# A hybrid decoder step on one core: the 16x16 diagonal blocks of a triangular inverse move from TensorE doubling steps to VectorE

## The chip, the cores and the metric

One Trainium2 chip, one of its cores. The metric is device time of one execution in microseconds (us); of several runs the median is given.

## The reference, cut to what matters

The kernel computes one inference step of a two-layer decoder trunk for 256 prompt rows and 8 sample rows. Each layer has a mixer (four mLSTM heads and eight gated-delta-rule heads behind one input projection), a cross attention and a SwiGLU. The part that the change touches is the chunked delta rule of the prompt:

```python
A = jnp.where(strict[None, :, :, None], decay_ts * kk * bc[:, None, :, :], 0.0)
eg = jnp.exp(g)
rhs = vc - eg[..., None] * jnp.einsum('bthd,bhde->bthe', kc, S)
U = lax.linalg.triangular_solve(jnp.transpose(A, (0, 3, 1, 2)), jnp.transpose(rhs, (0, 2, 1, 3)),
                                left_side=True, lower=True, unit_diagonal=True)
wu = bc[..., None] * jnp.transpose(U, (0, 2, 1, 3))
```

The system is unit lower triangular. The reference solves it in chunks of 64 rows; the kernel uses chunks of 128 rows, so that there are two chunks per head, and multiplies by an explicit inverse.

## The kernel before, in words

All weights stream from HBM in blocks of 128x1024 numbers. For each block `block` issues a DMA into `raw`; ScalarE (ACT) rounds it to `wh`; VectorE (DVE) forms the remainder `wl = raw - wh`; and `stream` on TensorE (PE) multiplies `wh` and `wl` with the rounded activations and their remainder (`xh`, `xl`), three matmuls of 264 columns for each pair of 128x128 tiles, 24 matmuls for a block. `wh` and `wl` have three buffers each, so a block can be prepared only once the block three before it is used up. These two operations carry a high priority.

Everything else of a layer runs as Python generators ("chains") beside these streams. A chain writes its next few instructions and yields a number; `pump`, called between the matmuls of a stream, resumes a chain once an estimated PE clock has passed that number of nanoseconds. PE's order is thus exactly the order in which the program writes its instructions (`manual_schedule`); each PE instruction stands in the stream where its chain was resumed, and PE waits there if its operands aren't ready. The orders on DVE, ACT and POOL are made by a scheduler at build time, from priorities and a timeline of its own; on the chip they are fixed too.

`gdn_prompt` is the chain of one pair of delta-rule heads: four groups in each of two layers, so eight calls. A call handles four 128x128 systems side by side (two heads by two chunks) in tiles of 128x512. It forms `N` (the strictly triangular matrix, transposed) on DVE, transposes `v` and `q` on PE (`vT`, `qT`), and then builds the inverse `Dm` and its transpose `Dt`. Before, `Dm` started as the identity. Its 2x2 blocks came from two DVE operations (lines L647 to L650, through the helper at L60, of the profile's kernel), `Dt` from a DVE block transposition (L651). Then the loop at L658 doubles the block size b from 2 to 64. At each level PE multiplies `A` (the transpose of `N`, made by four PE transpositions `NT` and one ACT copy) with the odd halves of `Dm` into `pp`; DVE masks that into `Pf`; PE multiplies by `Dt` into `pd`; DVE subtracts it from `Dm`, and for b up to 16 transposes again. For b up to 16, `pp` and `pd` are four fp32 matmuls of 128x64 each; at 32 and 64 they are smaller. Between the steps the chain yields 2100 and 1900 ns. In parallel other chains run: the conv and gates of the next group (`y`, `s`), the sample rows' state updates (`S`, `dS`, `wm`).

Of the kernel before, what the change touches and what calls it, by code (L numbers as in the profile page):

```python
# [8 lines left out]
F32 = mybir.dt.float32  # L9
F32R = mybir.dt.float32r  # L10
AF = mybir.ActivationFunctionType
ALU = mybir.AluOpType
AX = mybir.AxisListType
PSUM = bass.MemoryType.PSUM

P = 128
D = 2048
# [10 lines left out]
MEM = 256  # L28
EPS = 1e-6
WB, VB, SB, NV = 10, 6, 6, 6  # L30
PRIO = 1000
Q0, K0, V0, O0 = 0, 512, 1024, 2048
IF0 = 3072
# [5 lines left out]
def bc(ap, axis, n):  # L39

    a = ap.unsqueeze(axis)
    shape = list(a.shape)
    shape[axis] = n
    return a.to_broadcast(shape)
# [3 lines left out]
def kernel(ctx: ExitStack, tc: tile.TileContext, io: dict, outs: list):  # L48
    nc = tc.nc
    (y_p, y_s, p_C, p_n, p_m, p_S, p_conv, p_k, p_v, s_C, s_n, s_m, s_S, s_conv) = outs  # L50
    act, dve, pool, pe = nc.scalar, nc.vector, nc.gpsimd, nc.tensor

    def copy(out, in_, scale=1.0):
        act.activation(out, in_, AF.Copy, scale=scale)  # L54
# [4 lines left out]
    def tt(out, a, b, op, eng=None):  # L59
        (eng or dve).tensor_tensor(out=out, in0=a, in1=b, op=op)  # L60
# [41 lines left out]
    cp = ctx.enter_context(tc.tile_pool(name="const", bufs=1))  # L102
# [7 lines left out]
    def ps(name):  # L110
        return pm.tile([P, 512], F32, name=name, tag="m")


    ident = cp.tile([P, P], F32, name="ident")
# [24 lines left out]
                       channel_multiplier=1)  # L139

    up = {}
    b = 1
    while b < P:
        nb = P // (2 * b)
        m = cp.tile([P, nb], F32, name=f"up{b}")
        dve.memset(m, 1.0)
        pool.affine_select(out=m, in_=m, pattern=[[-2 * b, nb]], compare_op=ALU.is_ge, fill=0.0, base=0,
                           channel_multiplier=1)
        pool.affine_select(out=m, in_=m, pattern=[[2 * b, nb]], compare_op=ALU.is_ge, fill=0.0, base=b - 1,
                           channel_multiplier=-1)  # L150
        up[b] = m
        b *= 2

    twos = cp.tile([P, GH + MH], F32R, name="twos")
    dve.memset(twos.bitcast(F32), 0.0)
# [83 lines left out]
    def block(src, r0, nk, f0):  # L239
# [3 lines left out]
        lo = ring.tile([P, nk, fw], F32R, name="wl", tag="wl", bufs=3)  # L243
        with tc.high_priority(offset=PRIO):
            nc.sync.dma_start(out=raw, in_=src[r0:r0 + nk * P, f0:f0 + fw].rearrange("(k p) f -> p k f", p=P))
# [21 lines left out]
    def add_stream(src, r0, nk, hh, hl, nx=None, n=2):  # L267

        for g in range(KT // n):
            o = stream(src, r0, nk, g * n * P, lambda k: (hh[:, k], hl[:, k]), n)  # L270
            for j in range(n):
                t = n * g + j
                with tc.high_priority(offset=PRIO):
                    tt(xT[:, t], o[j], xT[:, t], ALU.add)
# [68 lines left out]
    def scaled(o, nx, out, k=1.0):  # L343

        with tc.high_priority(offset=PRIO):
            for j in range(len(o)):
# [36 lines left out]
    def gates(l, o, nx, mx, G, rstd):  # L383
        def gt(name):
            return mx.tile([P, C], F32, name=name, tag=name)

        def gtmp(name):
            return mx.tile([P, C], F32, name=name, tag="w", bufs=WB)

        while any(c is rstd for c in chains):  # L390
            yield 500.0
        with tc.high_priority(offset=PRIO):
            y, t1, ga, gl = gtmp("g_y"), gt("g_t1"), gtmp("g_a"), gtmp("g_l")
# [42 lines left out]
        yield 20000.0  # L436
        with tc.high_priority(offset=PRIO):
            pc = ps("pc")
# [32 lines left out]
        yield 8000.0  # L471
        with tc.high_priority(offset=PRIO):
            pt = ps("gT")
# [94 lines left out]
    def four(t):  # L568
        return t.rearrange("p (i t) -> p i t", i=4)
# [5 lines left out]
    def gdn_decay(g, G, M, R):  # L575
# [15 lines left out]
        yield 2400.0  # L591
        R.E, R.eL = E, eL

    def gdn_prompt(l, g, s, G, M, R):
        h0 = 2 * g
        q, k, v = s
# [29 lines left out]
        N, W = M.w("N"), M.w("W")  # L626
# [17 lines left out]
        power(qd, hm)  # L644

        Dm, Dt, A = M.w("Dm"), M.w("Dt"), M.w("A")
        pool.tensor_copy(out=Dm, in_=bc(ident, 1, 4))  # L647
        u = M.v("u", (4, 64))
        tt(u, N[:, :, 1::2], bc(up[1], 1, 4), ALU.mult)
        tt(Dm[:, :, 1::2], Dm[:, :, 1::2], u, ALU.subtract)  # L650
        dve.transpose(Dt.rearrange("p i t -> p (i t)"), Dm.rearrange("p i t -> p (i t)"))  # L651
        yield 2700.0
        pa = ps("NT")
        for i in range(4):
            tr(pa[:, i * P:(i + 1) * P], N[:, i])
        copy(A, four(pa))
        b = 2
        while b < P:  # L658
            def halves(t, which, i=None):
                x = t.rearrange("p i t -> p (i t)") if i is None else t[:, i]  # L660
# [37 lines left out]
        for c in range(2):  # L698
# [19 lines left out]
            w = M.v("wu")  # L718
# [33 lines left out]
        x = M.w("ox", (2, T))  # L752
# [338 lines left out]
    def mixers(l, nx, mx, st, nx2):  # L1091
# [26 lines left out]
        for g in range(4):  # L1118
            if g % 2 == 0:
                hs[g // 2] = hidden(f"gd{g}")  # L1120
            r = Run()
            r.z, r.E, r.at = None, None, 2 * (g % 2)
            r.formed, r.before = False, R[g - 1] if g else None
            r.hh, r.hl = hs[g // 2]
            R.append(r)
            S = st.tile([P, 2, NB, P], F32, name="S", tag="st")
            for j in range(2):
                nc.gpsimd.dma_start(out=S[:, j], in_=io["state_gdn_S"][l, :, 2 * g + j].rearrange("b k v -> k b v"))
            spawn(gdn_decay(g, G, M, r))
            if g == 0:  # L1130
                s = gdn_inputs(l, g, nx, cb, rawc, M, first)
            else:
                s = gdn_inputs(l, g, nx, cb, rawc, M)
            gd.append(spawn(gdn_prompt(l, g, s, G, M, r)))
            gd.append(spawn(gdn_sample(l, g, s, G, M, r, S, smp)))
            if g:
                gdn_z(l, g - 1, nx, M, R[g - 1])
# [315 lines left out]
    with tc.manual_schedule(engines={mybir.EngineType.PE}):  # L1453
# [25 lines left out]
        for c in range(3):  # L1479
            w = P if c < 2 else NB  # L1480
            mm(pr[:w, c:c + 1], nx.sa[0][:, c * P:c * P + w], ones[:, 0:1])
        for c in range(3):
            w = P if c < 2 else NB
# [3 lines left out]
        for q in range(4):  # L1487
            qs = slice(q * 512, (q + 1) * 512)
            for c in range(3):
                w = P if c < 2 else NB  # L1490
                o = nx.y[:w, c, qs]
                i = nx.pt[c][:w] if q == 3 else o
# [37 lines left out]
```

## Time and profile before

| | |
|---|---|
| Median of three runs | 3005.03 us (3001.89 to 3006.78) |
| The profiled execution, its own time | 3002.08 us |
| Its span, first to last instruction | 3000.4 us |
| ACT busy | 1467.5 us (49%) |
| POOL busy | 453.7 us (15%) |
| Mean granted TensorE clock | 0.996 |

An engine's busy share is the union of its instructions' time over the span. Matmuls are pipelined: one of 264 columns is listed with some 285 ns, but they start every 120 ns. In the timeline a row's first number is the start, the second the time that the row covers, and a bracket gives the idle time before it and what ended it. PE instructions in fp32 appear twice each, so that four matmuls make a row of eight. The delta-rule chains run from 90 to 380 us (layer 0) and from 1550 to 1860 us (layer 1) of the span.

### The profile page before, as it was taken

The numbers are of one execution on the slowest core, as the hardware profiler recorded it, in microseconds if no ns is written. First come the engines' busy times: TensorE is split into PE (matmuls) and PEld (weight loads), VectorE is DVE, ScalarE is ACT, GpSimd is POOL, SyncE is SP. The second block draws the span as 40 slices with busy tenths as digits, with TensorE's granted clock in tenths as the row PEclk, the third lists the DMA queues.
The fourth block names the chain that finished last, engine by engine and source line by source line (L and its number), as shares of the span: only waits on it lengthen the run. The fifth ranks groups of instructions, "written<-read, shape, count | busy, mean of one in ns | idle before, by whom it ended". The sixth has DMA issues, their size and how long they took to land.

```text
span 3000.4 us, 58120 instructions
## 1 busy us (share of the span) xinstructions
PE 2934.3 (98%) x23475; PEld 2856.3 (95%) x23475; DVE 2004.0 (67%) x3397; ACT 1467.5 (49%) x2441; POOL 453.7 (15%) x628
## 2 busy tenths in 40 slices
PE   8999999999999999999999999999999999999998
PEld 7999999978999999999999999999699999999998
DVE  7887676877555555555688777678775555555555
ACT  6555455556443333333465555556564333334335
POOL 5222100232100000000232221003220000000001
PEclk9999999999999999999999999999999999999999
DMA  7555465665666666666655554756656666666664
GB/s 199 148 145 150 146 192 172 218 210 180 184 182 179 181 182 179 181 182 178 179 160 157 150 157 133 221 157 211 225 170 182 181 179 182 181 179 182 180 180 134
DMA packets 381253, 530.10 MB, mean 177 GB/s; under 512 B 25576, under 2 KB 226224, under 8 KB 380960
## 3 DMA queue, kind: packets, MB, share of 16 engines
q1 hardware_dynamic: 363584, 498.47, 56.1%
q0 software_dynamic: 7424, 25.20, 2.7%
q10 hardware_dynamic: 9976, 2.72, 0.5%
q8 instruction: 184, 3.01, 0.4%
q14 instruction: 85, 0.70, 0.1%
HBM read 502.88 MB, written 23.83 MB: 176 GB/s over the span
## 4 chain that ended last, share of the span: by engine, by line
PE 43%; DVE 3%; ACT 2%; issue 1%; DMA 1%; POOL 0%; POOLq 0%; DVEq 0%; ACTq 0%
PE acc L72 37%; DVE wl L60 1%; PE kv L72 1%; PE pp L72 1%; PE pd L72 1%; PE dks L72 0%; DVE xl L57 0%; ACT wh L54 0%; DVE y L57 0%; PE dS L72 0%; PE sqC L72 0%; DVE xT L60 0%; PE pS L72 0%; POOL sa L60 0%; ACT wm L54 0%
## 5 line engine op out<-in xcount | busy, mean ns | idle before, releaser
L60 DVE TENSOR_TENSOR wl<-raw,wh 128x1024 fp32r<-128x1024 f32 x880 | 1088.2, 1237 | 803.0 <-ACT wh L54 801.7
L54 ACT ACTIVATE wh<-raw 128x1024 fp32r<-128x1024 f32 x880 | 931.1, 1059 | 1250.6 <-PE acc L72 1129.9
L72 PE MATMUL acc<-xh,wh 128*128 128x264 f32 x4736 | 1369.5, 289 | 5.8 <-ACT wh L54 3.5
L72 PE MATMUL acc<-xh,wl 128*128 128x264 f32 x4736 | 1350.7, 285 | 0.8 <-DVE wl L60 0.5
L72 PE MATMUL acc<-xl,wh 128*128 128x264 f32 x4736 | 1349.4, 285 | 1.1 <-DVE xl L57 1.1
L72 PEld LDWEIGHTS acc<-xh,wh 128*128 128x128 f32 x4736 | 896.2, 189 | 10.7 <-ACT wh L54 3.6
L72 PEld LDWEIGHTS acc<-xl,wh 128*128 128x128 f32 x4736 | 897.4, 189 | 4.2 <-DVE xl L57 1.7
L72 PEld LDWEIGHTS acc<-xh,wl 128*128 128x128 f32 x4736 | 895.6, 189 | 2.0 <-DVE wl L60 1.9
L72 PE MATMUL acc<-ffh,wh 128*128 128x264 f32 x1408 | 400.9, 285 | 0.6 <-DVE xT L60 0.4
L72 PE MATMUL acc<-ffl,wh 128*128 128x264 f32 x1408 | 400.9, 285 | 0.0
L72 PE MATMUL acc<-ffh,wl 128*128 128x264 f32 x1408 | 400.4, 284 | 0.0
L60 POOL TENSOR_TENSOR fg<-fg,rstd 128x264 f32<-128x264 f32 x88 | 95.4, 1112 | 1306.0 <-ACT fg L1412 1306.0
L72 PEld LDWEIGHTS acc<-ffh,wh 128*128 128x128 f32 x1408 | 264.9, 188 | 1.0 <-issue 0.9
L72 PEld LDWEIGHTS acc<-ffl,wh 128*128 128x128 f32 x1408 | 265.3, 188 | 0.0
L72 PEld LDWEIGHTS acc<-ffh,wl 128*128 128x128 f32 x1408 | 265.0, 188 | 0.0
L60 DVE TENSOR_TENSOR xT<-acc,xT 128x264 f32<-128x264 f32 x512 | 190.7, 423 | 18.9 <-PE acc L72 18.6
L60 POOL TENSOR_TENSOR sa<-sa,sq 128x264 f32<-128x264 f32 x96 | 95.6, 1014 | 250.2 <-ACT sq L313 249.9
L54 ACT ACTIVATE wm<-r,msk 72x128 fp32r<-72x128 f32 (+1 forms) x192 | 68.8, 426 | 20.4 <-PE dS L72 16.5
L57 DVE SCALAR_TENSOR_TENSOR xl<-xT,cst,xh 128x264 fp32r<-128x264 f32 x96 | 77.4, 841 | 0.6 <-ACT xh L54 0.5
L57 DVE SCALAR_TENSOR_TENSOR y<-y,cst,y 128x255 f32<-128x255 f32 (+1 forms) x144 | 63.0, 476 | 0.5
L54 ACT ACTIVATE xh<-xT,cst 128x264 fp32r<-128x264 f32 x80 | 39.6, 507 | 27.7 <-DVE xT L60 27.7
L60 DVE TENSOR_TENSOR y<-acc,rstd 128x264 f32<-128x264 f32 x96 | 37.8, 425 | 14.2 <-PE acc L72 9.8
(510 smaller groups left out, 3329.7 us busy)
## 6 DMA issues: line engine op xcount, KB each, us to landing
raw<-in_w_in_dram SPq DMA_DIRECT2D x224, 512.0 KB
raw<-in_ffn_w_gate_dram SPq DMA_DIRECT2D x176, 512.0 KB
raw<-in_ffn_w_up_dram SPq DMA_DIRECT2D x176, 512.0 KB
raw<-in_ffn_w_down_dram SPq DMA_DIRECT2D x176, 512.0 KB
raw<-in_w_out_dram SPq DMA_DIRECT2D x64, 512.0 KB
S<-in_state_gdn_S_dram POOLq DMA_DIRECT2D x16, 512.0 KB, 6.4
out_dram<-S SPq DMA_DIRECT2D x16, 512.0 KB
Ct<-in_state_mlstm_C_dram POOLq DMA_DIRECT2D x8, 1024.0 KB, 7.8
```

The costliest lines, as they stand in the source:

```text
L54: act.activation(out, in_, AF.Copy, scale=scale)
L57: dve.scalar_tensor_tensor(out=out, in0=a, scalar=s, in1=b, op0=o0, op1=o1)
L60: (eng or dve).tensor_tensor(out=out, in0=a, in1=b, op=op)
L72: pe.matmul(out=out, lhsT=lhsT, rhs=rhs, start=start, stop=stop)
```

## The change

Doubling now starts from blocks of 16 (`BASE = 16`). The 16x16 diagonal blocks of the inverse come from the new function `base_blocks`, which works without PE. ACT packs the four 32x32 diagonal squares of each system into a tile `u` of 128x128 (four copies of 32 partitions). In a second half of `u`, set to identity blocks by POOL, DVE solves column by column: for k = 15 down to 1 it multiplies the column k of `D` with row k of the block, spread over the partitions by 32x32 block transpositions (five of them, three rows each), and subtracts the product; each of these has 8 x k elements per partition. A last transposition, four ACT copies back into `Dm` and a full transposition into `Dt` end it. The chain's yields change with it: 5000 ns are added after the `NT` transpositions, and the yields of levels 2, 4 and 8 go.

```diff
+BASE = 16
...
-    b = 1
+    b = BASE
     while b < P:
         nb = P // (2 * b)
         m = cp.tile([P, nb], F32, name=f"up{b}")
...
+    eye = cp.tile([P, 32], F32, name="eye")
+    dve.tensor_reduce(out=eye, in_=ident.rearrange("p (n x) -> p x n", x=32), axis=AX.X, op=ALU.add)
...
+    def base_blocks(N, Dm, Dt, u):
+        Nc, D = u[:, 0], u[:, 1].rearrange("p (x i) -> p x i", i=BASE)
+        N3, room = Nc.rearrange("p (i t) -> p i t", i=4), Dt.rearrange("p i t -> p (i t)")
+        for r in range(0, P, 32):
+            copy(N3[r:r + 32], N[r:r + 32, :, r:r + 32])
+        pool.tensor_copy(out=u[:, 1].rearrange("p (a t) -> p a t", a=4), in_=bc(eye, 1, 4))
+        tmp = room[:, 3 * P:].rearrange("p (x i) -> p x i", i=BASE)
+        for k0 in range(BASE - 1, 0, -3):
+            ks = range(max(1, k0 - 2), k0 + 1)
+            w = len(ks)
+            src = Nc.rearrange("p (x k) -> p k x", k=BASE)[:, ks[0]:ks[0] + w]
+            dve.transpose(room[:, :w * P], bc(src, 3, BASE))
+            R = room[:, :w * P].rearrange("p (k x i) -> p k x i", k=w, i=BASE)
+            for k in reversed(ks):
+                tt(tmp[:, :, :k], bc(D[:, :, k], 2, k), R[:, k - ks[0], :, :k], ALU.mult)
+                tt(D[:, :, :k], D[:, :, :k], tmp[:, :, :k], ALU.subtract)
+        dve.transpose(Nc, u[:, 1])
+        for r in range(0, P, 32):
+            copy(Dm[r:r + 32, :, r:r + 32], N3[r:r + 32])
+        dve.transpose(room, Dm.rearrange("p i t -> p (i t)"))
...
         Dm, Dt, A = M.w("Dm"), M.w("Dt"), M.w("A")
-        pool.tensor_copy(out=Dm, in_=bc(ident, 1, 4))
-        u = M.v("u", (4, 64))
-        tt(u, N[:, :, 1::2], bc(up[1], 1, 4), ALU.mult)
-        tt(Dm[:, :, 1::2], Dm[:, :, 1::2], u, ALU.subtract)
-        dve.transpose(Dt.rearrange("p i t -> p (i t)"), Dm.rearrange("p i t -> p (i t)"))
+        pool.memset(Dm, 0.0)
+        base_blocks(N, Dm, Dt, M.v("u", (2, P)))
         yield 2700.0
         pa = ps("NT")
         for i in range(4):
             tr(pa[:, i * P:(i + 1) * P], N[:, i])
         copy(A, four(pa))
-        b = 2
+        yield 5000.0
+        b = BASE
         while b < P:
```

Two places show how the instructions move, both in the first call (layer 0, first pair of heads). The numbers behind names are buffers; they differ between the two builds.

The first is PE's order around the first `pp` of the call. Before, it is the level-2 product, 20 rows behind the `NT` transpositions (`wl_1525` is one weight block, `dS_1542` a product of the sample rows):

```order
L72 MATMUL acc0_1474<-xh_156,wl_1525 128x264
L72 MATMUL acc1_1475<-xh_156,wh_1524 128x264
L72 MATMUL acc1_1475<-xl_157,wh_1524 128x264
L72 MATMUL acc1_1475<-xh_156,wl_1525 128x264
L72 MATMUL pp_1535<-Dm_1424,A_1426 128x64 x4
L72 MATMUL dS_1542<-wm_1506,k3_223 128x512
L72 MATMUL acc0_1474<-xh_156,wh_1524 128x264
```

Now the first `pp` is the level-16 product, 64 rows behind `NT`:

```order
L73 MATMUL acc1_1504<-xh_142,wh_1595 128x264
L73 MATMUL acc1_1504<-xl_143,wh_1595 128x264
L73 MATMUL acc1_1504<-xh_142,wl_1596 128x264
L73 MATMUL dS_1624<-wm_1583,k3_209 128x512
L73 MATMUL pp_1635<-Dm_1410,A_1412 128x64 x4
L73 MATMUL acc0_1503<-xh_142,wh_1643 128x264
L73 MATMUL acc0_1503<-xl_143,wh_1643 128x264
L73 MATMUL acc0_1503<-xh_142,wl_1644 128x264
```

So the block with `wl_1596` is used up just ahead of `dS_1624` and `pp_1635`, and the next block, with `wl_1644`, begins right behind them.

The second is DVE's order where it works toward that `pp`. Before, the steps of the inverse stand singly between the weight blocks and the other chains (from the subtraction in the 2x2 blocks on):

```order
L60 TENSOR_TENSOR wl_1592<-raw_1590,wh_1591 128x1024
L57 SCALAR_TENSOR_TENSOR S_240<-S_240,gs_1128,dS_1500 128x128 x4
L57 SCALAR_TENSOR_TENSOR y_1456<-y0_1455,cst_149,y_1456 128x255
L60 TENSOR_TENSOR Dm_1424<-Dm_1424,u_1428 128x256
L643 TENSOR_SCALAR qd_1413<-qd_1413 128x4
L57 SCALAR_TENSOR_TENSOR y_1456<-y0_1455,cst_149,y_1456 128x255
L57 SCALAR_TENSOR_TENSOR y_1456<-y0_1455,cst_149,y_1456 128x254
L651 STREAM_TRANSPOSE Dt_1425<-Dm_1424 128x512
L60 TENSOR_TENSOR wl_1644<-raw_1642,wh_1643 128x1024
L812 TENSOR_SCALAR dq_1628<-dq_1628 8x2
```

Now, from the last weight block ahead of that `pp` on (`wl_1764`, three blocks behind `wl_1596`):

```order
L58 SCALAR_TENSOR_TENSOR S_226<-S_226,gs_1114,dS_1624 128x128 x4
L61 TENSOR_TENSOR u_1414<-u_1414,Dt_1411 128x8x14
L61 TENSOR_TENSOR wl_1764<-raw_1762,wh_1763 128x1024
L58 SCALAR_TENSOR_TENSOR s1_1500<-s1_1500,y_1485 128x528
L61 TENSOR_TENSOR dqn_1210<-dqn_1210,dq_1680 8x256
L61 TENSOR_TENSOR Dt_1411<-u_1414,Dt_1411 128x8x13
L61 TENSOR_TENSOR u_1414<-u_1414,Dt_1411 128x8x13
L611 STREAM_TRANSPOSE Dt_1411<-u_1414 128x384
L61 TENSOR_TENSOR Dt_1411<-u_1414,Dt_1411 128x8x12
L61 TENSOR_TENSOR u_1414<-u_1414,Dt_1411 128x8x12
```

Behind these rows the pairs go on down to k = 1 with three more transpositions and nothing else between them; then come the transposition of `u`, the one from `Dm` into `Dt`, and `Pf`, which reads `pp_1635`.

## The prediction

> **What bounds the kernel now.** I read the page's first part, then PE's groups by form, then the timelines around the first call, then the clock.
>
> ```profile
> span 3000.4 us, 58120 instructions
> PE 2934.3 (98%) x23475; PEld 2856.3 (95%) x23475; DVE 2004.0 (67%) x3397; ACT 1467.5 (49%) x2441; POOL 453.7 (15%) x628
> ```
>
> PE works without a gap for 98% of the span, so each matmul taken from its stream is time gained, and each wait put into it is time lost, one for one. DVE has room on average only; whether it has room where the new work stands must be read there.
>
> **What PE gives up.** The levels 2, 4 and 8 go.
>
> ```profile
> L72 PE MATMUL pp<-Dm,A 128*128 128x64 f32 x256 | 32.3, 269 | 3.8 <-DVE y L57 2.3 <-ACT A L54 1.5
> L72 PE MATMUL pd<-Pf,Dt 128*128 128x64 f32 x256 | 32.4, 270 | 0.1
> L72 PE MATMUL pp<-Dm,A 64*64 64x64 f32 x64 | 5.8, 235 | 1.1 <-DVE Dm L60 1.1
> L72 PE MATMUL pd<-Pf,Dt 64*64 64x64 f32 x64 | 5.6, 228 | 1.2 <-DVE Pf L674 1.2
> 119.74 0.28 PE L72 MATMUL acc<-xh,wl 128*128 128x264 f32 x1
> 119.86 1.00 PE L72 MATMUL pd<-Pf,Dt 128*128 128x64 f32 x8
> 120.67 0.37 PE L72 MATMUL acc<-xh,wh 128*128 128x264 f32 x1
> 120.87 0.28 PE L72 MATMUL acc<-xl,wh 128*128 128x264 f32 x1
> 120.99 0.28 PE L72 MATMUL acc<-xh,wl 128*128 128x264 f32 x1
> ```
>
> 256 records of eight per step are 32 steps `pp` and 32 `pd`: four levels by eight calls. Three of four levels go, so 48 steps. One costs what it shifts the stream by: without it the matmul at 120.87 would have started at 119.74 + 2 x 0.12 = 119.98, so 0.89 us. **48 x 0.89 = 42.7 us gained.** PE also waits 3.8 + 0.1 + 1.1 + 1.2 = 6.2 us in these groups; most of that stands at steps that go or that the new wait swallows, so I count 6 us as gained.
>
> **What DVE gives up and gets.**
>
> ```profile
> L691 DVE STREAM_TRANSPOSE Dt<-Dm 128x512 f32<-128x512 f32 x32 | 22.6, 706 | 0.5
> L60 DVE TENSOR_TENSOR Dm<-Dm,pd 128x256 f32<-128x256 f32 x32 | 13.3, 415 | 17.2 <-PE pd L72 16.8
> L60 DVE TENSOR_TENSOR kw<-kT,E 128x512 f32<-128x512 f32 x8 | 5.5, 685 | 4.7 <-ACT junk L612 4.7
> L693 DVE STREAM_TRANSPOSE Dt<-Dm 32x128 f32<-32x128 f32 x8 | 2.4, 300 | 0.2
> 350.26 0.16 DVE L914 TENSOR_SCALAR mrd<-mn 128x1 f32<-128x1 f32 x1
> 350.46 0.16 DVE L60 TENSOR_TENSOR mrd<-mn,mrd 128x1 f32<-128x1 f32 x1
> 350.65 0.16 DVE L60 TENSOR_TENSOR mrd<-mrd,em 128x2 f32<-128x2 f32 x1
> 350.84 0.17 DVE L917 RECIPROCAL mrd<-mrd 128x2 f32<-128x2 f32 x1
> ```
>
> Per call it gives up eight operations of 256 elements (0.415 each) and three transpositions of 0.706 net: 5.4 us, all off the path. It gets a chain in which each operation needs the one before. The rows at 350 show what such operations cost: 0.16 us long and starting every 0.195 us. An element adds (685 - 415)/256 = 1.06 ns. The pairs for k = 15 to 1 have 2 x 8 x 120 = 1920 elements: 30 x 0.195 + 2.0 = 7.9 us. The trace shows no transposition of 384 elements; between 0.300 (128) and 0.706 (512) it comes to 0.57. Five overlap their predecessor's tail by 0.07 and make 2.5 us. With the last 0.3 us the chain takes **10.7 us alone**. It has no cover of its own: the first `pp` of a call now needs all of it.
>
> **How long PE then stands at that pp.** The order of the first call gives a floor. Behind `wl_1764` there stand 26 small operations (k = 13 to 1), four transpositions, that of `u`, and two others. But `wl_1764` reuses the buffer of `wl_1596`, whose last matmul is two rows ahead of `pp`. So the following must fit in between while PE has one `dS` of 0.3 us to do:
>
> ```profile
> L54 ACT ACTIVATE wh<-raw 128x1024 fp32r<-128x1024 f32 x880 | 931.1, 1059 | 1250.6 <-PE acc L72 1129.9 <-issue 31.3 <-ACT fg L1412 16.8
> L60 DVE TENSOR_TENSOR wl<-raw,wh 128x1024 fp32r<-128x1024 f32 x880 | 1088.2, 1237 | 803.0 <-ACT wh L54 801.7
> L57 DVE SCALAR_TENSOR_TENSOR s<-s,y 128x528 f32<-128x528 f32 x24 | 16.7, 696 | 1.5 <-ACT s L828 1.5
> 100.93 2.46 ACT L54 ACTIVATE wm<-r,msk 72x128 fp32r<-72x128 f32 x8 [0.15 <-DVE r L60]
> ```
>
> ACT's `wh` 1.06 and DVE's `wl` 1.24 first. Then `s` 0.63 and a 256-element operation 0.35 (each less the 0.07 of overlap); 26 x 0.195 + 16 x 91 x 0.00106 = 6.6; transpositions 4 x 0.50 + 0.30 = 2.3, together 9.7 us with rounding and the overlaps. Then four ACT copies back into `Dm`: `wm` has the same 128 elements and takes 2.46/8 = 0.31, so 1.23 us. 1.06 + 1.24 + 9.7 + 1.23 - 0.3 = **12.9 us of standstill**. Doing the same from the last weight block in DVE's order of each call gives 12.9, 12.4, 12.4, 10.6, 9.3, 10.2, 10.1 and 4.9 us, **82.8 us** in all. It doesn't depend on how far DVE lags.
>
> A second sum starts from `N`.
>
> ```profile
> 91.61 1.16 PE L72 MATMUL kq<-s,s 128*128 128x128 f32 x8
> 102.72 1.13 DVE L57 SCALAR_TENSOR_TENSOR N<-kk,bs,E 128x128 f32<-128x128 f32 x4
> 1562.06 1.06 PE L72 MATMUL kq<-s,s 128*128 128x128 f32 x8
> 1565.92 1.13 DVE L57 SCALAR_TENSOR_TENSOR N<-kk,bs,E 128x128 f32<-128x128 f32 x4
> 1638.19 1.06 PE L72 MATMUL kq<-s,s 128*128 128x128 f32 x8
> 1649.44 1.11 DVE L57 SCALAR_TENSOR_TENSOR N<-kk,bs,E 128x128 f32<-128x128 f32 x4
> 105.96 1.22 DVE L60 TENSOR_TENSOR wl<-raw,wh 128x1024 fp32r<-128x1024 f32 x1
> 107.11 1.11 DVE L57 SCALAR_TENSOR_TENSOR S<-S,gs,dS 128x128 f32<-128x128 f32 x4
> ```
>
> In the first call DVE begins `N` 11.1 us after PE began `kq`. From `N` to the last base row DVE now has 70 rows: 36 of the chain (10.1 us where others stand between them) and 34 others (four `wl` at 1.15, see 105.96 to 107.11, twelve `N` and `S` at some 0.27, `y`, `W`, `vn` and the like), 24.6 us. PE has 20.4 us from the end of `kq` to `pp` (150 `acc` at 0.1208, the rest transpositions and `dS`). 11.1 - 0.93 (the `kq` itself) + 24.6 + 1.23 - 20.4 = 15.6 us. With the starts of `N` that the trace shows, 3.9 (1562.06 to 1565.92) to 11.3 us (1638.19 to 1649.44) behind `kq`, the eight calls make 106 us; with 5 us for the calls that now follow a standstill, in which DVE catches up, 90 us. Between 82.8 and 106 I take **90 us**, since six of the eight calls start behind such a standstill.
>
> **What a standstill does to the clock.** PE's clock column in the table by stages, and PE's timeline at the same place:
>
> ```profile
> 292.00:294.00 2.00, 0.17 (x2) 0.00 (x0) 1.88 (x4) 0.41 (x3) 0.00 (x0) 0.89 0.15 37
> 294.00:304.00 10.00, 9.67 (x47) 8.89 (x48) 3.79 (x10) 5.36 (x15) 0.00 (x0) 0.51 0.38 106
> 304.00:306.00 2.00, 2.00 (x20) 1.93 (x18) 1.55 (x2) 0.43 (x1) 0.00 (x0) 1.00 0.87 246
> 2088.00:2092.00 4.00, 4.00 (x23) 4.00 (x22) 1.38 (x3) 3.50 (x5) 0.00 (x0) 0.62 0.50 169
> 294.33 0.80 PE L72 MATMUL dS<-wm,k 72*128 72x512 f32 x1 [2.15 <-ACT wm L54]
> 295.14 0.42 PE L72 MATMUL acc<-xl,wh 128*128 128x264 f32 x1
> 295.36 0.42 PE L72 MATMUL acc<-xh,wl 128*128 128x264 f32 x1
> ```
>
> After only 2.15 us without work PE gets half its clock for the 10 us that follow (0.51), and matmuls start every 0.22 instead of 0.12 us: 10 x (1 - 0.12/0.22) = 4.5 us lost. Around 2088 us it is short: a mean of 0.62 over 4 us is 3 us at half, 1.4 us lost. A standstill of some 10 us should do the same each time. I take 2.5 us, between the two and nearer the short one, since PE has unbroken work behind `pp`: 8 x 2.5 = **20 us** (11 to 36). The Trainium skill ("TensorE: Matmul & The Clock Gate", section "What's actually happening") says that the clock halves after about 3.4 us of idleness and comes back after about 3.4 us of sustained work; an estimate by that page is 8 x 3.4 x 0.45 = 12 us, a sum of 3055 us. The trace agrees on the half, but shows it after a shorter pause and once for three times as long, and the measurement decides.
>
> **The sum**, made against the profiled execution of 3002.08 us, 3 us below the median: 3002.1 - 42.7 - 6 + 90 + 20 = **3063 us**, slower by 2.0%.
>
> **Rivals.**
> - *The chain hides, and PE's gain stays.* Then 3002.1 - 42.7 - 6, with some 16 us for short waits, gives 2970 us. It decides at a standstill of 48.7/8 = 6 us a call, where the clock is left out. For it: DVE is free a third of the time, and PE has 20 us between `kq` and `pp`, twice the chain alone. Against: the trace has DVE full there, and behind the last weight block nothing but the chain stands in its order. It would need operations at 0.08 us instead of 0.195, and still more. Chance 0.07.
> - *Break-even*: both halves too large, about 3003 us. Chance 0.03.
> - *The standstill without the clock's loss*: 3043 us; the row at 2088 speaks for a small loss, that at 294 against none. Chance 0.12.
> - *DVE stays late behind pp*: `Dt`, `Pf`, the `S` updates and the conv stand ahead of the next weight block, so PE could run out of blocks; at 5 us a call, 40 us more: 3103 us. Against: three blocks are ready at `pp`, 8.7 us of PE work. Chance 0.13.
> - *The change isn't carried out as written*: the built order shows both sides of it, so I give it nothing.
>
> The forecast has 0.65. **The range** reaches from the floor with chain operations as cheap as independent ones (26 x 0.115 = 3 us less a call: 82.8 - 24 + 11 of clock, 3023 us) to 106 + 36 with the later wait of 1 us a call (3104 us, rounded). Faster by over 0.2% (what a measurement of this kernel can tell from no change): 0.07; within 0.2%: 0.03; slower: 0.90.
>
> **What the profile would show.** PE: 64 records each of `pp` and `pd` at 128x64; idle before `pp` of some 10 us eight times, released by ACT's copy into `Dm`; half clock behind each. DVE: operations of 8k elements every 0.2 us or a little more, 10 to 11 us of chain a call. If `pp` starts without a wait, the order of DVE wasn't what decides, and I am wrong in sign; if the waits are there but the small operations take 0.1 us, I am wrong in size.

## The result, and the profile after

Slower, as forecast. The changed kernel takes 3081.93 us (median of 4 runs, 3080.14 to 3086.45) against 3003.53 us (4 runs, 3001.89 to 3006.78): 1.0268 times the time before, with a 95% interval of 1.0255 to 1.0281. The forecast was 3063 us, 19 us too low and inside its range. In one execution of an experiment below, `m12_ordered`, PE ran at half speed throughout and the kernel took 5701.75 us; that execution is left out.

The page's first part and its row of the clock, after:

```profile
span 3080.0 us, 57582 instructions
PE 2914.5 (95%) x23091; PEld 2836.6 (92%) x23091; DVE 2033.6 (66%) x3594; ACT 1484.9 (48%) x2505; POOL 450.4 (15%) x628
PEclk9898899999999999999999899999999999999999
```

PE has 384 records less and 20 us less of busy time, but the span is 79.6 us longer than the 3000.4 us before. DVE's share fell from 67 to 66%, although it got 197 instructions more: by the profile's page alone nothing is crowded.

PE's groups by form, with idle time and its releasers last:

```profile
L73 PE MATMUL pp<-Dm,A 128*128 128x64 f32 x64 | 15.5, 424 | 97.1 <-issue 49.8 <-ACT Dm L55 47.3
L73 PE MATMUL pd<-Pf,Dt 128*128 128x64 f32 x64 | 8.2, 271 | 0.0
L73 PE MATMUL acc<-xh,wl 128*128 128x264 f32 x4736 | 1356.6, 286 | 1.1 <-DVE wl L61 0.9
```

The 48 steps are gone (64 records each where there were 256), and PE now stands 97.1 us ahead of `pp`. The mean `pp` matmul takes 424 instead of 269 ns; the clock column below shows it at half clock. Behind the standstills PE doesn't run out of weight blocks: 1.1 us of waits for `wl` in 4736 matmuls.

PE's waits (total us, times, longest):

```profile
PE pp L73 <- issue: 49.8, 4, 13.5
PE pp L73 <- ACT Dm L55: 47.3, 4, 15.2
```

That is eight waits, one for each call: 15.2, 13.2, 13.5, 11.7, 11.8, 12.4, 12.2 and 7.2 us by PE's timeline. For four of them the trace shows no releaser ("issue"). All eight end 1.4 to 1.5 us behind the last transposition of the chain, of which ACT's four copies take 1.26.

The first of them in the timeline (start, duration, engine, line):

```profile
117.10 0.40 PE L73 MATMUL dS<-wm,k 72*128 72x512 f32 x1
117.90 1.21 DVE L61 TENSOR_TENSOR wl<-raw,wh 128x1024 fp32r<-128x1024 f32 x1
119.11 1.10 DVE L58 SCALAR_TENSOR_TENSOR S<-S,gs,dS 128x128 f32<-128x128 f32 x4
120.33 1.21 DVE L61 TENSOR_TENSOR wl<-raw,wh 128x1024 fp32r<-128x1024 f32 x1
121.46 0.69 DVE L58 SCALAR_TENSOR_TENSOR s<-s,y 128x528 f32<-128x528 f32 x1
...
122.41 0.25 DVE L61 TENSOR_TENSOR Dt<-u,Dt 128x104 f32<-128x104 f32 x1
122.70 0.28 DVE L61 TENSOR_TENSOR u<-u,Dt 128x104 f32<-128x104 f32 x1
...
129.64 0.18 DVE L61 TENSOR_TENSOR Dt<-u,Dt 128x24 f32<-128x24 f32 x1
129.85 0.18 DVE L61 TENSOR_TENSOR u<-u,Dt 128x24 f32<-128x24 f32 x1
130.07 0.17 DVE L61 TENSOR_TENSOR Dt<-u,Dt 128x16 f32<-128x16 f32 x1
...
130.91 0.31 DVE L616 STREAM_TRANSPOSE u<-u 128x128 f32<-128x128 f32 x1
131.25 1.26 ACT L55 ACTIVATE Dm<-u 32x128 f32<-32x128 f32 x4 [12.28 <-DVE u L616]
132.66 1.94 PE L73 MATMUL pp<-Dm,A 128*128 128x64 f32 x8 [15.15 <-ACT Dm L55]
```

`dS` is PE's last work before `pp`. From the `s` behind the last weight block (121.46) to the end of the transposition of `u` (130.91 + 0.31 = 131.22) DVE does nothing but the chain, `s` and one other operation, and PE has nothing to do.

The same place in the table by stages, after (length, then busy time and count of PE, PEld, DVE, ACT and POOL, then PE's clock, the DMA share and GB/s):

```profile
107.20:131.25 24.05, 10.30 (x83) 9.88 (x81) 23.12 (x70) 11.67 (x35) 4.27 (x8) 0.75 0.49 143
118.00:132.50 14.50, 0.00 (x0) 0.00 (x0) 12.32 (x41) 2.19 (x6) 1.34 (x3) 0.55 0.43 123
132.50:136.50 4.00, 3.84 (x18) 3.87 (x19) 1.14 (x2) 0.02 (x1) 0.00 (x0) 0.50 0.00 0
136.50:140.00 3.50, 3.50 (x30) 3.46 (x30) 1.37 (x6) 0.49 (x1) 0.00 (x0) 1.00 0.00 0
```

From the start of `N` to the end of the chain DVE is busy 23.12 of 24.05 us, while PE is busy for 10.30. Its share of 66% is a mean over stages; here it is 96%, the chain included, and over the same stretch of all eight calls 91% (200.4 of 219.4 us). And behind the restart PE works at half clock for some 4 us.

The balance of the two traces: the time in which PE isn't busy grew from 3000.4 - 2934.3 = 66.1 to 3080.0 - 2914.5 = 165.5 us, by 99.4 us. 92.2 of them are ahead of `pp` (from 5.0 to 97.2, all sizes of `pp` together), 7.2 at other places. The clock column is at half while PE is busy for 16.3 us before and 62.3 us after, of which 1 - 0.12/0.22 is lost: 7.4 and 28.3 us, 20.9 us more. 99.4 + 20.9 - 42.7 for the steps makes 77.6 of the 79.6 us.

### The profile page after: what moved, and what is told of

Its sections match the earlier page's. It is cut to its first block, busy times and chain, and to the rows that moved or that the text cites. A ratio compares the mean times of both kernels' runs of the same rounds, so it can differ in the third digit from the quotient of the medians.

```text
span 3080.0 us, 57582 instructions
## 1 busy us (share of the span) xinstructions
PE 2914.5 (95%) x23091; PEld 2836.6 (92%) x23091; DVE 2033.6 (66%) x3594; ACT 1484.9 (48%) x2505; POOL 450.4 (15%) x628
## 5 line engine op out<-in xcount | busy, mean ns | idle before, releaser
L73 PE MATMUL pp<-Dm,A 32*32 32x32 f32 (+2 forms) x256 | 24.4, 259 | 97.2 <-issue 49.8
L73 PEld LDWEIGHTS pp<-Dm,A 32*32 32x32 f32 (+2 forms) x256 | 21.2, 169 | 101.3 <-issue 99.2
L55 ACT ACTIVATE wm<-r,msk 72x128 fp32r<-72x128 f32 (+1 forms) x192 | 68.5, 426 | 17.1 <-PE dS L73 15.2
```

What stands on the lines that cost most here:

```text
L73: pe.matmul(out=out, lhsT=lhsT, rhs=rhs, start=start, stop=stop)
```

## The experiments

Three theories were open on why PE waits. **A**: the chain just starts too late or its reader comes too soon, so moving one against the other saves the wait. **B**: DVE has no room for the chain between `N` and `pp`; whatever is done first, something that PE needs comes late. **C**: there is room, but DVE's built order leaves the dependent chain for last, behind the weight blocks. All times are against the kernel before on the same chip, and "after" is the changed kernel, of which each is an edit.

### Moving the chain and its reader (A)

`e2_late12` puts `pp` later in PE's order:

```diff
-        yield 5000.0
+        yield 12000.0
         b = BASE
```

> Edit: the new yield behind the NT transpositions is 12000 instead of 5000 ns, so PE meets the first pp about 7.6 us later (7000 estimated ns at 0.1208 us for 110 ns). Theory A (PE waits only because the serial chain on DVE has not ended): each of the eight standstills shrinks by about 7.6 us, 97 us to about 37 us in all, time about 3020 us. Rival B (DVE has no room in these stages, so the missing time only moves to later waits): total PE idle falls by less than 20 us, time 3060 us or more.

3050.28 us, ratio 1.0158 (1.0143 to 1.0173). PE's group:

```profile
L73 PE MATMUL pp<-Dm,A 128*128 128x64 f32 x64 | 15.5, 424 | 75.0 <-ACT Dm L55 53.9 <-issue 21.1
```

The waits shrank by 22 us, not by some 60, and the time lies between what A and B expected: neither gave the number. In the built order more weight blocks now stand between the first and the last operation of the chain, 5 to 8 in place of 3 to 5. With the later reader DVE takes in more other work in between.

`e5_early` starts the chain before the first pause behind `N` (the added lines stand right behind `W`, ahead of `yield 4500.0`):

```diff
+        Dm, Dt, A = M.w("Dm"), M.w("Dt"), M.w("A")
+        pool.memset(Dm, 0.0)
+        base_blocks(N, Dm, Dt, M.v("u", (2, P)))
...
-        Dm, Dt, A = M.w("Dm"), M.w("Dt"), M.w("A")
-        pool.memset(Dm, 0.0)
-        base_blocks(N, Dm, Dt, M.v("u", (2, P)))
         yield 2700.0
```

> Edit: base_blocks is written right behind W, ahead of the yields of 4500 and 1600 ns, with nothing else changed, so the chain may start up to 6.6 us earlier against PE's order. Theory A: standstills shrink by 4 to 6.6 us each, 97 to about 45-65 us, time about 3030-3050 us. Rival B: the other DVE work that the chain then displaces stands in the way of PE instead; time 3070 us or more.

3070.08 us, 1.0224 (1.0209 to 1.0239), with 87.1 us of waits at `pp`, only 10 less. The timeline of its first call:

```profile
108.48 0.57 DVE L611 STREAM_TRANSPOSE Dt<-u 128x384 f32<-128x384 f32 x1
...
127.99 0.31 DVE L616 STREAM_TRANSPOSE u<-u 128x128 f32<-128x128 f32 x1
...
129.74 1.94 PE L73 MATMUL pp<-Dm,A 128*128 128x64 f32 x8 [15.14 <-ACT Dm L55]
```

The chain takes 19.8 us (19.0 after) instead of the 10.7 that it needs alone, since other work stands among it, and the first wait is as long as after (15.14 against 15.15). But the edit hardly started the chain earlier. Its first transposition comes 2.5 to 4.2 us behind the start of `N` in the eight calls, where it came 3.7 to 6.6 us behind it after: 1.7 us earlier in the mean, not the 4 to 6.6 that A reckoned with. So this run doesn't show what a really earlier start would be worth.

`e7_early_late120` does both:

> Edit: both, base_blocks written right behind W and the yield at 12000 ns, some 14 us of room more than in the changed kernel. Theory A: nearly all of the 97 us of standstill goes, and with it about 18 us of half clock behind them; time about 2965-2980 us, faster than before the change by the 43 us of matmuls less what little waits remain. Rival B: the time only moves, 3030 us or more. Rival C (the longer chain is exposed where the layer's streams end): PE idle grows there by over 10 us, time about 2990 us.

3047.24 us, 1.0146 (1.0129 to 1.0163), 71.3 us at `pp`. A falls as far as the reader goes: some 7 us more for it, with a start earlier by little, leave three quarters of the wait. Still later places, and a start much nearer to `N`, weren't tried.

### Making the chain shorter

`e3_no_low_columns` leaves out the multiplications and subtractions of the columns 7 to 1 (14 of the 30), with order and transpositions as they are:

```diff
             for k in reversed(ks):
+                if k <= 7:
+                    continue
```

> Edit: the multiplications and subtractions of the columns k = 7 to 1 are left out (14 of 30 small operations; part of the inverse is missing); transpositions, copies, PE's order and all yields stay. These operations stand at the end of the chain in seven of eight calls. By the rows of before they cost 14 x 0.195 + 448 x 0.00106 = 3.2 us a call: if they are all on the path of pp, standstills fall by 26 us, from 97 to 71, time about 3052 us. If the standstill is set by other work, less than 8 us.

3053.22 us, 1.0166 (1.0151 to 1.0181). PE's group:

```profile
L73 PE MATMUL pp<-Dm,A 128*128 128x64 f32 x64 | 14.7, 406 | 69.7 <-issue 37.4 <-ACT Dm L55 32.3
```

The waits fell by 97.1 - 69.7 = 27.4 us. In seven calls each fell by 3.0 to 3.2 us, 14 operations at some 0.22 us, which is about the spacing that the timeline shows (0.21 us at 129.64, 0.29 at 122.41): what leaves the end of the chain leaves the wait in full. In the eighth the wait fell from 7.2 to 1.3 us, more than these operations explain. So the end of the chain does set the time at `pp`.

`e4_base8` makes the blocks 8x8; PE does one level more:

```diff
-BASE = 16
+BASE = 8
```

> Edit: BASE = 8, so the chain on DVE has 7 columns instead of 15 and three row transpositions instead of five, and PE does the level 8 again. Theory A: the chain is 16 operations (4.2 us) and two transpositions (1.0 us) shorter, so eight standstills shrink by about 5 us each (97 to about 57 us); PE gets 16 steps of 0.89 us back (14 us); time about 3055 us. Rival B (other DVE work sets the standstill): standstills stay above 85 us, time about 3090 us.

3042.88 us, 1.0131 (1.0116 to 1.0146). PE's group:

```profile
L73 PE MATMUL pp<-Dm,A 128*128 128x64 f32 x128 | 23.5, 346 | 50.0 <-issue 34.3 <-ACT Dm L55 15.7
```

Half the columns and half the waits, and the time is better than expected. Giving 16 steps back to PE (14 us) pays, but the kernel before stays ahead.

### Another order on DVE (C)

`m5_ordered` ties each of the next weight blocks, in order alone, behind a group of three columns, so that the chain can't be left for last:

```diff
+    marks = []
...
-            split(h, lo, raw)
+            mark = marks.pop(0) if marks else None
+            if mark is None:
+                split(h, lo, raw)
+            else:
+                with tc.issue_after(mark):
+                    split(h, lo, raw)
...
-                tt(D[:, :, :k], D[:, :, :k], tmp[:, :, :k], ALU.subtract)
+                i = dve.tensor_tensor(out=D[:, :, :k], in0=D[:, :, :k], in1=tmp[:, :, :k], op=ALU.subtract)
+            marks.append(getattr(i, "ins", i))
```

> Edit: the changed kernel with one thing added: the remainder wl of each of the five weight blocks that follow base_blocks is issued on DVE behind one group of three columns (an order-only edge), so the chain can no longer be left until DVE has nothing else. Same work, same place of pp on PE. Theory C (the chain is last in DVE's order, since after each of its dependent operations something else is ready first; it runs only once PE stands and the other work has dried up): standstills at pp fall from 97 to 15-45 us, time 3000-3025 us. Theory B (DVE has no room for the chain before pp, in whatever order): total PE idle stays above 120 us, shifted to waits for wl; time 3065 us or more.

3092.2 us, 1.0293 (1.0278 to 1.0308): slower than after, as B expected. PE's groups:

```profile
L73 PE MATMUL acc<-xh,wl 128*128 128x264 f32 x4736 | 1365.6, 288 | 50.6 <-DVE wl L61 50.4
L73 PE MATMUL pp<-Dm,A 128*128 128x64 f32 x64 | 15.5, 424 | 43.7 <-issue 28.4 <-ACT Dm L55 15.3
```

The wait at `pp` halved, and as much came up at the weight blocks, which PE didn't wait for before. C falls for this place of `pp` and this set of edges.

`m12_ordered` has the edges and `yield 12000.0`:

> Edit: the same order edges, and the yield at 12000 ns. Theory C: no standstill over 2 us at the eight pp, PE idle back to some 55 us, half clock as before the change; the matmuls given up stay as gain: 3003.5 - 42.7 + 5 to 15 = 2966-2976 us. Theory B: over 3030 us, as without the edges (3050 us).

3030.2 us in the middle of four executions (3025.59 to 3033.94), ratio 1.0088 (1.0069 to 1.0106). The profile is that of one more run of the same kernel, `m12_again`:

> Edit: none against m12_ordered, whose profile showed an execution at another clock and can't be compared; this is a second look at its waits. Time as measured before, about 3030 us. Theory B (room on DVE): the standstills at pp are gone or below 2 us, and in their place PE waits 25-45 us in all for weight blocks (acc) in the stretches before pp, since DVE is full there. Theory C (order alone): PE idle is back to some 55 us and the rest of the time is half clock.

3029.76 us, beside 3001.09 for the kernel before. PE's groups:

```profile
L73 PE MATMUL acc<-xh,wl 128*128 128x264 f32 x4736 | 1358.3, 287 | 52.2 <-DVE wl L61 52.0
L73 PE MATMUL pp<-Dm,A 128*128 128x64 f32 x64 | 8.0, 268 | 0.0
```

Nothing waits at `pp` any more, and the kernel is still 29 us behind the one before: 52 us went to the weight blocks, more than the 25 to 45 that B expected. The timeline of the first call, and its row of the table by stages from the start of `N` to `pp`:

```profile
101.77 1.13 DVE L58 SCALAR_TENSOR_TENSOR N<-kk,bs,E 128x128 f32<-128x128 f32 x4
...
105.95 0.58 DVE L618 STREAM_TRANSPOSE Dt<-u 128x384 f32<-128x384 f32 x1 [1.01 <-ACT u L55]
106.56 0.28 DVE L61 TENSOR_TENSOR Dt<-u,Dt 128x120 f32<-128x120 f32 x1
...
110.36 1.20 DVE L61 TENSOR_TENSOR wl<-raw,wh 128x1024 fp32r<-128x1024 f32 x1
111.61 0.59 PE L73 MATMUL acc<-xh,wl 128*128 128x264 f32 x1 [6.91 <-DVE wl L61]
...
101.77:133.62 31.85, 23.80 (x170) 23.03 (x169) 29.57 (x83) 18.57 (x48) 7.93 (x14) 0.84 0.40 121
```

With three columns done first, the next weight block comes at 110.36, and PE has stood 6.91 us for it. DVE is busy for 29.57 of the 31.85 us. Order is worth something (20 us against `e2_late12`, which has the same place of `pp`), but these edges didn't make room: C expected 2966 to 2976 us and falls for them too. They weren't the best possible either: the chain ended 3.6 to 6.2 us ahead of `pp`, where ACT's copies need 1.3, so a part of the 52 us may be the edges' own.

`m8_base8_ordered` is the same with blocks of 8x8 and `yield 8000.0`:

> Edit: BASE = 8, the same order edges, yield 8000 ns. Theory C: standstills gone, 32 instead of 48 steps given up on PE: 3003.5 - 28.5 + 0 to 10 = 2975-2985 us. Theory B: over 3020 us.

3023.9 us, 1.0068 (1.0053 to 1.0083): 0.2 us of waits at `pp`, 38.8 at the weight blocks. C expected 2975 to 2985 and falls; the edges stood closer than this place of `pp` needed, since each chain ended 8 to 14 us ahead of it, so a part of the 38.8 us may be the edges' own.

### Taking the chain off DVE

`p16_pool` is `e7_early_late120` with the multiplications and subtractions on POOL:

```diff
-                tt(tmp[:, :, :k], bc(D[:, :, k], 2, k), R[:, k - ks[0], :, :k], ALU.mult)
-                tt(D[:, :, :k], D[:, :, :k], tmp[:, :, :k], ALU.subtract)
+                tt(tmp[:, :, :k], bc(D[:, :, k], 2, k), R[:, k - ks[0], :, :k], ALU.mult, pool)
+                tt(D[:, :, :k], D[:, :, :k], tmp[:, :, :k], ALU.subtract, pool)
```

> Edit: BASE = 16, base_blocks written right behind W, yield 12000 ns (as in e7_early_late120, 3047 us), and the 30 multiplications and subtractions on POOL. POOL's operations of 8 to 264 elements took 0.4 to 1.1 us before, so 30 of them take some 18 us and the chain with its transpositions some 22-28 us, where PE gives it some 25. Theory B: waits at pp of 0 to 4 us a call, time 2970-3000 us. Theory C: 3035 us or more.

3020.89 us, 1.0068 (1.0052 to 1.0085). Its rows for PE's `pp` and for POOL:

```profile
L73 PE MATMUL pp<-Dm,A 128*128 128x64 f32 x64 | 13.7, 386 | 44.2 <-ACT Dm L55 34.6 <-issue 9.5
L61 POOL TENSOR_TENSOR Dt<-u,Dt 128x120 f32<-128x120 f32 (+14 forms) x120 | 62.4, 520 | 24.9 <-DVE Dt L611 14.3 <-DVE qd L673 2.9 <-issue 2.2
L61 POOL TENSOR_TENSOR u<-u,Dt 128x120 f32<-128x120 f32 (+14 forms) x120 | 50.7, 422 | 8.0
```

Between the expectations (3000 and 3035 us). By the ratios it is 0.78% or 23 us faster than the same chain at the same place on DVE, and the waits at `pp` are 71.3 - 44.2 = 27.1 us shorter, though POOL needs 0.42 to 0.52 us for an operation: DVE's room was worth more than the operation's speed. 30 such operations alone take POOL 14 us, and so `pp` still waits.

`p8_pool_base8` is the same with `BASE = 8` and `yield 8000.0`:

> Edit: BASE = 8, base_blocks written right behind W, yield 8000 ns, and the 14 multiplications and subtractions of the chain on POOL instead of DVE (transpositions and copies stay). Theory B (the engine that forms the weight remainders has no room between N and pp: in the runs so far DVE was idle there for 0 to 5 of 20 to 38 us): with the columns on an engine that is busy 15% of the time, PE's waits at pp and for weight blocks fall below 2 us a call; the 32 steps given up stay as gain, 28.5 us, half clock as before the change; time 2978-2992 us. Theory C (a serial chain is always too late, on whatever engine): waits of 5 us or more a call, time 3010 us or more.

2995.74 us (11 runs, 2993.93 to 3001.38), ratio 0.9982 (0.9973 to 0.9991). PE's group:

```profile
L73 PE MATMUL pp<-Dm,A 128*128 128x64 f32 x128 | 18.2, 290 | 14.4 <-ACT Dm L55 8.2 <-issue 5.7 <-DVE Dm L61 0.5
```

Slower than the 2978 to 2992 us that B expected: two calls still wait longer than its 2 us, 7.3 and 5.7.

`b4_base4` leaves all on DVE, behind `W`, with `BASE = 4` and `yield 4000.0`, a chain of six small operations:

> Edit: BASE = 4, base_blocks right behind W, yield 4000 ns, all on DVE. The chain is 6 small operations and one row transposition, about 3.3 us with the rest; DVE gives up 3.9 us (the 2x2 blocks, level 2 and two transpositions), so its load is not above that before the change. PE gives up 16 steps, 14.2 us. Theory B: no new waits, 2988-2994 us. Theory C: the tail of the chain still stands behind everything else, waits of 2 us or more a call, 3003 us or more.

2994.02 us (10 runs, 2991.56 to 2995.36), ratio 0.9976 (0.9967 to 0.9985). PE's group:

```profile
L73 PE MATMUL pp<-Dm,A 128*128 128x64 f32 x192 | 25.2, 276 | 8.4 <-issue 7.5 <-POOL kqf L789 1.0
```

That is B's time (2988 to 2994), though the first call alone still waits 6.7 us. Both are faster than the kernel before, by 0.18 and 0.24%. For `b4_base4` the balance closes: 16 steps less make 14.2 us; `pp` gives back 8.4 - 5.0, and the half clock 3.7 us (11.1 lost against 7.4), which leaves 7.1 us, against 6.7 us of span (3000.4 to 2993.7). The idea of the change holds where the chain is short enough for DVE's room; here DVE's busy time is no longer than before (2002.0 against 2004.0 us), so nothing was added to it.

## Why the prediction was right in sign and 19 us low

- **PE's 48 steps, 42.7 us.** Right: the records are gone, and with this term the balance closes to 2 us.
- **6 us of waits as gained.** Wrong. The 5.0 us at `pp` went, but PE's other waits grew by 7.2 us. The prediction counted the waits that go and asked nowhere what would be late next among them.
- **9.7 us of the chain and its neighbours behind the last weight block.** Right: the first call shows 121.46 to 131.22, 9.76 us. The transposition of 384 elements, interpolated at 0.57, takes 0.57; dependent small operations start every 0.21 to 0.22 us (129.64, 129.85, 130.07), with the 1.06 ns for each element inside.
- **90 us of standstill.** Too small: 97.1. The floor holds as a lower bound in all eight calls, and the wait is longer by as much as DVE lags. It gave 12.9 us for the first and the trace has 15.15: `dS` ends at 117.50 and the last `wl` begins at 120.33, 2.8 us later, where the floor allowed 1.06 - 0.3 = 0.76 us for ACT's `wh` alone. In that time DVE did another `wl` (117.90) and four `S`: it lagged, by 2.1 us. Over the eight calls this and the like cost 97.1 - 82.8 = 14.3 us, 1.8 us each.
- **The cut from 106 to 90.** The second sum had the lag, and for the first call it is close (15.6 against 15.15). It was cut on the ground that DVE catches up in a standstill, so that `N` begins 5 us behind `kq` in the six calls that follow one. This step failed. After the change those six begin 4.0 to 11.2 us behind, 50.5 us in all where the cut reckoned with 30. The second call, with the longest delay:

```profile
173.02 1.06 PE L73 MATMUL kq<-s,s 128*128 128x128 f32 x8
184.27 1.11 DVE L58 SCALAR_TENSOR_TENSOR N<-kk,bs,E 128x128 f32<-128x128 f32 x4
```

So the second sum was too high for another reason, which stays open, since it isn't worked out call by call, and 90 came near to 97.1 in part by luck: a cut of 9 would have been right, but not for this reason.
- **20 us of clock loss.** 20.9. The half clock behind each restart is there (0.50, then 1.00 from 136.5 us). Behind the eight standstills it costs 2.2 us each (39.2 us of work at half clock, last section) against the 2.5 forecast; the remaining 3 us are other stretches at half clock.
- **The sum.** Against the profiled execution of 3081.7 us 18.7 us are missing. 15 of them are the waits and the standstill together: -6 + 90 = 84 forecast, 99.4 measured. 1 us is the clock's, and 2 us are those that the balance doesn't place.
- **The rivals.** Chain hidden (2970) and break-even (3003): excluded by eight waits and 78 us. A standstill without clock loss (3043): excluded by the 20.9 us. DVE late behind `pp` (3103): 1.1 us at the weight blocks, so not here; under `m5_ordered`, where the chain goes first, waits for weight blocks are the result, but ahead of `pp`.

What the experiments add is the reason. The prediction worked with DVE's order ("behind the last weight block nothing but the chain stands in its order"), which explains where the wait shows. That the chain's end sets it is shown by `e3_no_low_columns`, where the waits shrink nearly one for one with the operations left out. The orders of `m5_ordered` and `m12_again` move the wait to the weight blocks, and a later reader (`e2_late12`, `e7_early_late120`) leaves most of it. Fewer operations on DVE remove a good part: 27 of 71 us in `p16_pool`. That DVE has little room there can be read in the trace of before, from the start of `N` for as long as PE took after the change to come from `N` to `pp` (the first call, then the sum of the eight):

```profile
102.72:113.04 10.32, 7.99 (x65) 7.70 (x65) 10.32 (x27) 8.13 (x28) 4.36 (x7) 1.00 0.48 135
sum 133.73, PE 129.60 PEld 128.57 DVE 118.52 ACT 75.05 POOL 37.22; mean PE 16.20 PEld 16.07 DVE 14.81 ACT 9.38 POOL 4.65
```

DVE was free for 133.73 - 118.52 = 15.2 us in all eight, none of it in the first. An estimate from this: with all that the change takes off DVE (5.4 us a call by the prediction, 43 us) there are 58.4 us for a chain of 8 x 10.1 = 80.8 us, so some 22 of the 97 us have no room unless other work on DVE is put off. How the rest divides between room and order stays open, and so does how much a perfect order on DVE could save at 16x16: the best one tried, 3030 us, was still 0.9% over the kernel before.

## What to carry to other kernels

A free third of an engine is no room for a serial chain: read the engine's busy share, before the change, between the chain's input and its reader (here 118.5 of 133.7 us), and count what else that engine must deliver there. Each standstill of the bounding engine costs clock besides (here 20.9 us on 97), so a new wait in its stream costs more than its length. Where a step moves work from the bounding engine, try the smallest portion first: one level of the four, with the chain written earlier, gained 0.24% where three lost 2.7%.

## What the hardware showed that I had not expected

- The clock loss hardly depends on how long the standstill is. Behind the eight standstills of the changed kernel PE works at half clock for 3.7 to 6.1 us: 3.9 us behind the longest (15.2 us), 3.7 behind the shortest (7.2). The sum of the table by stages over these eight stretches, each of them at a clock of 0.50:

```profile
sum 39.83, PE 39.22 PEld 39.26 DVE 10.26 ACT 1.70 POOL 0.17; mean PE 4.90 PEld 4.91 DVE 1.28 ACT 0.21 POOL 0.02
```

That is 4.9 us a restart. In `e3_no_low_columns` the waits fell by 27.4 us and the time by 3081.9 - 3053.2 = 28.7 us, so its restarts cost about as much behind shorter waits. The Trainium skill ("TensorE: Matmul & The Clock Gate", section "What's actually happening") gives about 3.4 us of sustained work until the clock is back. This trace comes near to that at its shortest (3.7 us) and is well above it at its longest (6.1 us).
- Operations of 8 to 120 elements on POOL take 0.42 to 0.52 us in the mean where DVE's start every 0.21 to 0.29 us, a factor of about two, and single ones up to 2.2 us, as the view of that tile in `p8_pool_base8` shows:

```profile
L61 POOL TENSOR_TENSOR Dt<-u,Dt x56: 244/404/2240, 111.2 to 1806.4; 128x112 f32<-128x112 f32 x8, 128x96 f32<-128x96 f32 x8, 128x80 f32<-128x80 f32 x8, 128x64 f32<-128x64 f32 x8
```

The three numbers are the shortest, the median and the longest in ns.
